# Rotary embedding from cached tables: the sums of one row block move from TensorE to POOL, the first store follows them, and the spread table halves are copied whole

## The chip, the cores and the metric

The kernel runs on one core of a Trainium2 chip. A core has TensorE (PE in the profile, with its weight loads as PEld), VectorE (DVE), ScalarE (ACT), GpSimd (POOL) and SyncE (SP), which here only issues transfers, and 16 DMA engines that all transfers share. The metric is device time in microseconds (us), the median of several executions. A profile is a record of one more execution; its span runs from the first to the last recorded instruction, and the execution's own time is a little longer.

## The reference

`x` has shape (8, 8, 1024, 64) in float32: 8 x 8 heads, 1024 positions, 64 channels. `cos_cached` and `sin_cached` have one row of 32 values for each position.

```
x_first, x_second = x[..., :32], x[..., 32:]
out_first  = x_first * cos - x_second * sin
out_second = x_first * sin + x_second * cos
out = concatenate([out_first, out_second], axis=-1)
```

So each half of each row is multiplied by both tables, and the four products are combined in two sums. Input and output have 16.8 MB each, the tables 0.13 MB each.

## The kernel before, in words

**Tiles.** `x` is cut into 8 tiles x0 to x7 of 128 partitions by 4096 elements (2 MB). A partition holds 64 rows of 64 channels, so 16 partitions in a row cover the 1024 positions of one head, and the tables needed repeat every 16 partitions. All eight tiles stay in SBUF, and results are written in place. `s` is a second tile of the same size (three buffers in turn) for the sine products.

**Loads.** SP issues the sine table and then all of x, in order: x0 in two halves, x1 to x7 whole (lines 55 to 63). ScalarE's queue takes the cosine table (line 56). The transfers report on a small set of semaphores that are used in turn, so that a later transfer can have to wait until the earlier one with the same semaphore has landed.

**Tables.** `sn` and `cs` must hold, in every partition, the 64 table rows which its 64 rows of x need. They are loaded into `raw` as 32 blocks of 32 rows, one block (1024 elements) to a partition. A partition of x needs two neighbouring blocks: an even one for its rows 0 to 32, an odd one for its rows 32 to 64. The odd blocks come from a shuffle on DVE and six copies of 32 partitions on POOL and ScalarE (lines 136 to 141). The even table blocks are spread to 128 partitions by matmuls with the 0/1 matrix `sel` into PSUM (line 134): four matmuls of 512 columns, sine and cosine for rows 0 to 16 (half 0 of the block), then for rows 16 to 32 (half 1). Each result is a PSUM tile of its own: n0, c0, n1, c1.

**The first tile, x0.** Its rows 0 to 32 are multiplied by DVE with the tables straight from those PSUM tiles (lines 142 to 146): four products, s and x for rows 0 to 16, then for rows 16 to 32. ScalarE meanwhile copies rows 32 to 64 of x0 to PSUM (`stage`, tiles pre0 and pre1) and then the four PSUM tables to `sn` and `cs` (lines 150 to 152). DVE multiplies the staged rows with `products`. The sums of rows 16 to 32, 32 to 48 and 48 to 64 are made by POOL (`pool_sums`), in that order; those of rows 0 to 16 are left to TensorE.

**The rest.** x2 is computed by POOL alone (`on_pool`, twice 32 rows). Tiles 1, 3, 4, 5, 6 and 7 are cut into chunks of 24, 24 and 16 rows: 18 chunks, 0 to 17. For each, ScalarE copies x to PSUM (`stage`, two staging tiles `st` in turn), and DVE makes both products (`products`). The sums are made in one of three ways:

- by DVE itself, for the chunks in `alone`;
- by POOL (`pool_sums`), for those in `behind`;
- by TensorE (`pe_sums`), in groups of 16 rows, ten of them in `on_pe`: four matmuls with plus or minus the unit matrix add the products in the one PSUM tile `acc`, and ScalarE copies the result back to x (`pe_back`).

**Order.** The order on each engine is written out by hand. In the loop over the chunks (lines 205 to 214), chunk c's products are written first, then the staging copy of chunk c + 2, then, if c is in `back_after`, the copy back of the TensorE group that is running and the matmuls of the next, and last what stands for c in `behind`: stores and POOL sums. A group's matmuls need `acc`, so they wait for the copy back of the group before. ScalarE thus alternates between staging copies, which wait for DVE to be done with a staging tile, and copies back, which wait for TensorE.

**Stores.** x0, x1 and the last quarter of x7 go out on ScalarE's queue, x2 to x6 and the rest of x7 on SP's. A store waits on its queue for all parts of its tile, and what is behind it on that queue waits with it. "Store 0" below is that of x0, and so on.

Of the kernel before, what the change touches and what calls it, by code (L numbers as in the profile page):

```python
# [8 lines left out]
def kernel(  # L9
# [7 lines left out]
    nc = tc.nc  # L17
    fp32 = mybir.dt.float32
    TT = mybir.AluOpType
    P = nc.NUM_PARTITIONS  # L20
# [7 lines left out]
    BK = 512  # L28
    G = BK // half
    Q = 32  # L30
    H = R // 2
    C = H * half
# [13 lines left out]
    cs = const.tile([P, T], fp32, name="cs")  # L46
    sn = const.tile([P, T], fp32, name="sn")
    sel = const.tile([Q, P], fp32, name="sel")
# [27 lines left out]
    def rows(t, n0, n1):  # L76
        return t[:, n0 * hd:n1 * hd].rearrange("p (n k j) -> p n k j", k=2, j=half)

    def tab(t, n0, n1):
        v = t[:, n0 * half:n1 * half].rearrange("p (n o j) -> p n o j", o=1, j=half)  # L80
        return v.to_broadcast([P, n1 - n0, 2, half])

    def mul(eng, o, a, t):
        eng.tensor_tensor(out=o, in0=a, in1=t, op=TT.mult)  # L84

    def sums(eng, o, c, s):
        eng.tensor_tensor(out=o[:, :, 0], in0=c[:, :, 0], in1=s[:, :, 1], op=TT.subtract)  # L87
        eng.tensor_tensor(out=o[:, :, 1], in0=c[:, :, 1], in1=s[:, :, 0], op=TT.add)  # L88
# [3 lines left out]
    def s_of(u):  # L92
        if u not in sv:
            sv[u] = tv.tile([P, F], fp32, name="s", tag="s")
        return sv[u]

    def stage(pt, u, n0, n1):
        nc.scalar.copy(out=pt[:, :(n1 - n0) * hd], in_=xt[u][:, n0 * hd:n1 * hd])  # L98

    def products(pt, u, n0, n1, alone=False):  # L100

        xr, sr, pr = rows(xt[u], n0, n1), rows(s_of(u), n0, n1), rows(pt, 0, n1 - n0)
        mul(nc.vector, sr, pr, tab(sn, n0, n1))
        mul(nc.vector, pr if alone else xr, pr, tab(cs, n0, n1))
        if alone:
            sums(nc.vector, xr, pr, sr)
# [8 lines left out]
    def pool_sums(u, n0, n1):  # L115
        xr = rows(xt[u], n0, n1)
        sums(nc.gpsimd, xr, xr, rows(s_of(u), n0, n1))

    def store(q, u, n0=0, n1=R):
        q.dma_start(out=of[u][:, n0 * hd:n1 * hd], in_=xt[u][:, n0 * hd:n1 * hd])  # L120
# [5 lines left out]
    with ExitStack() as first:  # L126
        p0, p1, p2 = [first.enter_context(tc.tile_pool(name=n, bufs=1, space=PS))
                      for n in ("p0", "p1", "p2")]
        even = [[p0.tile([P, BK], fp32, name="n0"), p0.tile([P, BK], fp32, name="n1")],
                [p0.tile([P, BK], fp32, name="c0"), p1.tile([P, BK], fp32, name="c1")]]  # L130
        pre = [p1.tile([P, 2 * BK], fp32, name="pre0"), p2.tile([P, 2 * BK], fp32, name="pre1")]
        for i in range(2):
            for part, r in zip(even, (rs, rc)):
                nc.tensor.matmul(part[i], sel, r[:, i * BK:(i + 1) * BK],  # L134
                                 start=True, stop=True)
        odd = [2 * (i % (Q // 2)) + 1 for i in range(Q)]
        for t, r in ((sn, rs), (cs, rc)):
            nc.vector.stream_shuffle(t[0:Q, C:], r, odd)  # L138
        for t, k, eng in ((sn, 1, 0), (sn, 2, 1), (sn, 3, 0), (cs, 1, 1), (cs, 2, 0), (cs, 3, 1)):
            f = nc.gpsimd.tensor_copy if eng else nc.scalar.copy  # L140
            f(out=t[k * Q:(k + 1) * Q, C:], in_=t[0:Q, C:])  # L141
        for i in range(2):
            n0, n1 = i * G, (i + 1) * G
            xr = rows(xt[0], n0, n1)
            mul(nc.vector, rows(s_of(0), n0, n1), xr, tab(even[0][i], 0, G))
            mul(nc.vector, xr, xr, tab(even[1][i], 0, G))
        pool_sums(0, G, H)
        for i in range(2):
            stage(pre[i], 0, H + i * G, H + (i + 1) * G)
        for i in range(2):  # L150
            for t, part in ((sn, even[0]), (cs, even[1])):
                nc.scalar.copy(out=t[:, i * BK:(i + 1) * BK], in_=part[i])
        for i in range(2):
            n0, n1 = H + i * G, H + (i + 1) * G
            products(pre[i], 0, n0, n1)
            pool_sums(0, n0, n1)
# [7 lines left out]
    def pe_sums(u, n0):  # L164
        xr, sr = rows(xt[u], n0, n0 + G), rows(s_of(u), n0, n0 + G)
        for k in range(2):
            nc.tensor.matmul(a[:, k], plus, xr[:, :, k], start=True, stop=False)  # L167
            nc.tensor.matmul(a[:, k], plus if k else minus, sr[:, :, 1 - k],  # L168
                             start=False, stop=True)

    def pe_back(u, n0):
# [7 lines left out]
    cuts = ((0, 24), (24, 48), (48, 64))  # L179
    chunks = [(u, n0, n1) for u in (1, 3, 4, 5, 6, 7) for n0, n1 in cuts]  # L180
    alone = {(1, 48), (5, 48), (7, 24), (7, 48)}
    on_pe = [(0, 0), (1, 0), (1, 16), (1, 32), (3, 0), (3, 16), (4, 0), (4, 16), (5, 0), (6, 0)]
    back_after = (0, 1, 3, 5, 6, 8, 10, 11, 13, 15)
    behind = {
        0: [(store, nc.scalar, 0)],
        5: [(store, nc.scalar, 1), (pool_sums, 3, 32, 64)],
        8: [(store, nc.sync, 3), (pool_sums, 4, 32, 64)],
        10: [(pool_sums, 5, 16, 48)],
# [8 lines left out]
    def put(c):  # L197
        if c < len(chunks):
            u, n0, n1 = chunks[c]
            stage(st[c % 2], u, n0, n1)  # L200

    put(0)
    put(1)
    pe_sums(*on_pe[0])
    for c, (u, n0, n1) in enumerate(chunks):
        products(st[c % 2], u, n0, n1, (u, n0) in alone)
        put(c + 2)
        if c in back_after:
            i = back_after.index(c)
# [34 lines left out]
```

## Time and profile before

| What | Value |
|---|---|
| Time, median of 6 executions | 86.93 us (86.51 to 87.24) |
| The profiled execution's own time | 87.03 us |
| Its span | 84.2 us |
| DVE busy | 71.2 us (85%) |
| POOL busy | 63.5 us (75%) |
| PE busy | 47.7 us (57%) |
| ACT busy | 41.7 us (49%) |
| Bytes moved by DMA | 33.83 MB, mean 402 GB/s |
| DVE's last instruction | starts at 75.60 us, 0.68 us long |
| Issue of stores 0 and 1 | 23.85 and 38.57 us |
| Issue of stores 2 to 6 | 47.76, 52.38, 60.68, 65.48 and 70.28 us |
| Issue of the two stores of x7 | 72.75 and 76.31 us |

Busy time is time with an instruction in execution on an engine. In lists of instructions in order of time a line gives the start, the duration, the engine, the line of the kernel, the operation, what is written and read, the number of merged records, and in brackets the idle time before it with what ended it. The row by slices has 40 slices of the span; a digit is the busy share in tenths, 9 standing for 90% or more.

### The profile page before, as it was taken

To read this page: it belongs to the slowest core of one execution; us is meant where nothing else is said; L and a number is where in the kernel's file an instruction comes from. 1 tells how busy PE (TensorE), PEld (TensorE's weight loads), DVE (VectorE), ACT (ScalarE), POOL (GpSimd) and SP (SyncE) were. 2 spreads that over 40 slices of the span, in tenths; PEclk is the share of its full clock that TensorE was granted. 3 is DMA by queue.
4 is the path that set the end of the run, shared out by engine and by line. 5 is a ranking of instruction groups with operands and counts; after the bars stand their busy time and mean duration, and the time that the engine had idled before them with its cause. 6 is when DMAs were issued, how large, how long until landed. Compare 5 with 4: busy or idle time off the path is not lost.

```text
span 84.2 us, 434 instructions
## 1 busy us (share of the span) xinstructions
PE 47.7 (57%) x88; PEld 18.2 (22%) x88; DVE 71.2 (85%) x56; ACT 41.7 (49%) x39; POOL 63.5 (75%) x37
## 2 busy tenths in 40 slices
PE   0199920089769494966949496299495980000000
PEld 0143200034133241413324141134140420000000
DVE  0198879999999999999999999999999999992000
ACT  4359795903372964685288544660675763000000
POOL 5049009999999999999999999999979999400000
PEclk9999999999999999999999999955999999655555
DMA  2999999999989999999999999999999999999980
GB/s 31 304 416 463 405 436 436 420 451 389 475 381 381 358 444 420 436 436 420 444 412 459 412 459 389 459 412 444 428 428 436 420 447 405 451 420 422 438 364 18
DMA packets 2691, 33.83 MB, mean 402 GB/s; under 512 B 321, under 2 KB 321, under 8 KB 513
## 3 DMA queue, kind: packets, MB, share of 16 engines
q1 hardware_dynamic: 2208, 28.97, 82.5%
q10 hardware_dynamic: 480, 4.85, 13.6%
q14 instruction: 3, 0.02, 0.0%
HBM read 17.04 MB, written 16.78 MB: 401 GB/s over the span
## 4 chain that ended last, share of the span: by engine, by line
DVE 47%; issue 2%; ACT 1%; DVEq 1%
DVE s L84 21%; DVE x L84 18%; DVE st L84 5%; DVE x L87 2%; DVE x L88 2%; ACT st L98 1%; DVEq L239 1%
## 5 line engine op out<-in xcount | busy, mean ns | idle before, releaser
L167 PE MATMUL acc<-x,plus 128*128 128x512 f32 x40 | 23.4, 670 | 17.5 <-ACT x L172 11.4
L98 ACT COPY st<-x 128x1536 f32<-128x1536 f32 (+1 forms) x18 | 23.4, 1302 | 13.3 <-DVE x L84 10.2
L84 DVE TENSOR_TENSOR s<-st,sn 128x1536 f32<-128x1536 f32 (+1 forms) x18 | 28.3, 1570 | 0.0
L84 DVE TENSOR_TENSOR x<-st,cs 128x1536 f32<-128x1536 f32 (+1 forms) x14 | 22.9, 1634 | 0.0
L87 POOL TENSOR_TENSOR x<-x,s 128x512 f32<-128x512 f32 (+2 forms) x9 | 16.3, 1814 | 4.4 <-issue 4.0
L88 POOL TENSOR_TENSOR x<-x,s 128x512 f32<-128x512 f32 (+2 forms) x9 | 16.3, 1809 | 0.0
L172 ACT COPY x<-acc 128x1024 f32<-128x1024 f32 x10 | 10.1, 1011 | 10.9 <-PE acc L168 10.9
L167 PEld LDWEIGHTS acc<-x,plus 128*128 128x128 f32 x40 | 7.6, 210 | 32.4 <-ACT x L172 18.9
L168 PE MATMUL acc<-s,minus 128*128 128x512 f32 x20 | 12.0, 685 | 0.0
L168 PE MATMUL acc<-s,plus 128*128 128x512 f32 x20 | 10.2, 593 | 0.0
L84 POOL TENSOR_TENSOR x<-x,cs 128x2048 f32<-128x2048 f32 x2 | 9.1, 4543 | 0.2
L84 POOL TENSOR_TENSOR g<-x,sn 128x2048 f32<-128x2048 f32 x2 | 9.1, 4544 | 0.1
L134 PE MATMUL n<-raw,sel 32*128 32x512 f32 x4 | 3.9, 1089 | 3.9 <-DMA raw<-in_sin_cached_dram 3.9
L84 DVE TENSOR_TENSOR st<-st,cs 128x1024 f32<-128x1024 f32 (+1 forms) x4 | 5.4, 1356 | 0.0
L168 PEld LDWEIGHTS acc<-s,minus 128*128 128x128 f32 x20 | 4.2, 211 | 5.3 <-issue 5.3
L168 PEld LDWEIGHTS acc<-s,plus 128*128 128x128 f32 x20 | 4.0, 198 | 5.3 <-issue 5.3
L87 POOL TENSOR_TENSOR x<-x,g 128x1024 f32<-128x1024 f32 x2 | 4.7, 2354 | 0.2
L88 POOL TENSOR_TENSOR x<-x,g 128x1024 f32<-128x1024 f32 x2 | 4.7, 2354 | 0.0
L134 PE MATMUL c<-raw,sel 32*128 32x512 f32 x4 | 3.8, 1056 | 0.0
L141 POOL COPY sn<-sn 32x1024 f32<-32x1024 f32 x1 | 1.0, 1029 | 3.4 <-DVE sn L138 3.4
L141 ACT COPY sn<-sn 32x1024 f32<-32x1024 f32 x2 | 2.1, 1043 | 2.4 <-DVE sn L138 2.4
L138 DVE LOAD_MASK_SELECT sn<-raw x1 | 0.0, 14 | 3.8 <-DMA raw<-in_sin_cached_dram 3.8
(26 smaller groups left out, 31.3 us busy)
## 6 DMA issues: line engine op xcount, KB each, us to landing
x<-in_x_dram SPq DMA_DIRECT2D x7, 2048.0 KB, 26.6
out_dram<-x SPq DMA_DIRECT2D x5, 2048.0 KB, 8.0
out_dram<-x ACTq DMA_DIRECT2D x2, 2048.0 KB, 13.8
x<-in_x_dram SPq DMA_DIRECT2D x2, 1024.0 KB, 6.3
out_dram<-x SPq DMA_DIRECT2D x1, 1536.0 KB, 9.7
out_dram<-x ACTq DMA_DIRECT2D x1, 512.0 KB, 6.9
raw<-in_cos_cached_dram ACTq DMA_DIRECT2D x1, 128.0 KB, 3.4
raw<-in_sin_cached_dram SPq DMA_DIRECT2D x1, 128.0 KB, 3.1
```

The costliest lines, as they stand in the source:

```text
L84: eng.tensor_tensor(out=o, in0=a, in1=t, op=TT.mult)
L87: eng.tensor_tensor(out=o[:, :, 0], in0=c[:, :, 0], in1=s[:, :, 1], op=TT.subtract)
L88: eng.tensor_tensor(out=o[:, :, 1], in0=c[:, :, 1], in1=s[:, :, 0], op=TT.add)
L98: nc.scalar.copy(out=pt[:, :(n1 - n0) * hd], in_=xt[u][:, n0 * hd:n1 * hd])
L134: nc.tensor.matmul(part[i], sel, r[:, i * BK:(i + 1) * BK], start=True, stop=True)
L141: f(out=t[k * Q:(k + 1) * Q, C:], in_=t[0:Q, C:])
L167: nc.tensor.matmul(a[:, k], plus, xr[:, :, k], start=True, stop=False)
L168: nc.tensor.matmul(a[:, k], plus if k else minus, sr[:, :, 1 - k], start=False, stop=True)
L172: nc.scalar.copy(out=rows(xt[u], n0, n0 + G), in_=a.rearrange("p k n j -> p n k j"))
L239: with _tile.TileContext(nc) as tc:
```

## The change

Four things change:

- The spread sine and cosine blocks are one PSUM tile each (`n` and `c`, 1024 columns) instead of four tiles. The matmuls of half 0 are written ahead of DVE's products as before, those of half 1 behind DVE's products and POOL's sums for rows 0 to 16 (`spread`).
- POOL also makes the sums of rows 0 to 16 of x0, ahead of its others. The TensorE group (0, 0) is gone from `on_pe`, with its copy back; the matmuls of (1, 0) are started behind chunk 0.
- ScalarE copies each spread table in one instruction of 1024 columns instead of two of 512.
- Store 0 is written ahead of the loop over chunks, behind the first two staging copies on ScalarE. It then waits for POOL's sums alone, not for a copy back.

In the built program the matmuls of half 1 wait for DVE: the sine one for the first of DVE's products, the cosine one for the second. The load of x7, which waited for the second half of x0's load, now waits for x1's load, and the load of x4 waits for the cosine table's.

```diff
-        even = [[p0.tile([P, BK], fp32, name="n0"), p0.tile([P, BK], fp32, name="n1")],
-                [p0.tile([P, BK], fp32, name="c0"), p1.tile([P, BK], fp32, name="c1")]]
-        pre = [p1.tile([P, 2 * BK], fp32, name="pre0"), p2.tile([P, 2 * BK], fp32, name="pre1")]
-        for i in range(2):
+        even = [p0.tile([P, C], fp32, name=n) for n in "nc"]
+        pre = [p.tile([P, 2 * BK], fp32, name="pre") for p in (p1, p2)]
+
+        def spread(i):
             for part, r in zip(even, (rs, rc)):
-                nc.tensor.matmul(part[i], sel, r[:, i * BK:(i + 1) * BK],
+                nc.tensor.matmul(part[:, i * BK:(i + 1) * BK], sel, r[:, i * BK:(i + 1) * BK],
                                  start=True, stop=True)
...
+        spread(0)
         for i in range(2):
             n0, n1 = i * G, (i + 1) * G
             xr = rows(xt[0], n0, n1)
-            mul(nc.vector, rows(s_of(0), n0, n1), xr, tab(even[0][i], 0, G))
-            mul(nc.vector, xr, xr, tab(even[1][i], 0, G))
-        pool_sums(0, G, H)
+            mul(nc.vector, rows(s_of(0), n0, n1), xr, tab(even[0], n0, n1))
+            mul(nc.vector, xr, xr, tab(even[1], n0, n1))
+            pool_sums(0, n0, n1)
+            if i == 0:
+                spread(1)
         for i in range(2):
             stage(pre[i], 0, H + i * G, H + (i + 1) * G)
-        for i in range(2):
-            for t, part in ((sn, even[0]), (cs, even[1])):
-                nc.scalar.copy(out=t[:, i * BK:(i + 1) * BK], in_=part[i])
+        for t, part in ((sn, even[0]), (cs, even[1])):
+            nc.scalar.copy(out=t[:, :C], in_=part)
...
-    on_pe = [(0, 0), (1, 0), (1, 16), (1, 32), (3, 0), (3, 16), (4, 0), (4, 16), (5, 0), (6, 0)]
-    back_after = (0, 1, 3, 5, 6, 8, 10, 11, 13, 15)
+    on_pe = [(1, 0), (1, 16), (1, 32), (3, 0), (3, 16), (4, 0), (4, 16), (5, 0), (6, 0)]
+    back_after = (1, 3, 5, 6, 8, 10, 11, 13, 15)
     behind = {
-        0: [(store, nc.scalar, 0)],
+        0: [(pe_sums, 1, 0)],
...
     put(0)
     put(1)
-    pe_sums(*on_pe[0])
+    store(nc.scalar, 0)
     for c, (u, n0, n1) in enumerate(chunks):
```

## The prediction

> **What bounds the kernel now.** I read the chain of waits first. It ends on DVE and gives it 47% of the span, which would make VectorE the bound. The row by slices of the page does not agree:
>
> ```profile
> span 84.2 us, 434 instructions
> ...
> DVE  0198879999999999999999999999999999992000
> ...
> DMA  2999999999989999999999999999999999999980
> GB/s 31 304 416 463 405 436 436 420 451 389 475 381 381 358 444 420 436 436 420 444 412 459 412 459 389 459 412 444 428 428 436 420 447 405 451 420 422 438 364 18
> ```
>
> DVE stops about six slices before the end; the DMA engines are at 9 from the second slice to the last but one. Nothing idles on that side until the bytes are through: 33.83 MB at some 430 GB/s is 78.7 us, and with 1.7 us before the first packet and about 2 us from the last packet to the span's end that is nearly all of 84.2. The edges, in the table by stretches (us, then busy time of PE, PEld, DVE, ACT, POOL, then TensorE clock, DMA share, GB/s):
>
> ```profile
> 26.00:28.00 2.00, 1.53 (x4) 0.38 (x2) 2.00 (x3) 0.43 (x1) 2.00 (x1) 1.00 1.03 295
> 60.00:62.00 2.00, 1.34 (x3) 0.68 (x4) 2.00 (x3) 1.55 (x3) 1.55 (x1) 1.00 1.01 434
> 76.00:82.00 6.00, 0.00 (x0) 0.00 (x0) 0.28 (x1) 0.00 (x0) 0.00 (x0) 0.50 0.97 408
> 82.00:83.00 1.00, 0.00 (x0) 0.00 (x0) 0.00 (x0) 0.00 (x0) 0.00 (x0) 0.50 0.17 66
> ```
>
> From 76.3 us on no engine computes, and the DMA engines still work off a backlog until just past 82.
>
> So a change moves the end only if it makes the DMA engines idle, starts them at another time, or changes what a byte costs. Where are they near to idling? Stores 4, 5 and 6 (tiles x4, x5, x6) are issued at 60.68, 65.48 and 70.28 by SP, and the stores ahead of them land at 63.4, 68.2 and 73.5. Store 3's sixteen closing packets (under 512 B) pass between 62.25 and 63.0, so its data ends there, 62.6 in the mean. An issue needs 1.0 us to its first packet: the first one starts at 0.74, and in the DMA view of 1 to 3 us (0.05 us a digit) the first busy digit stands at 1.75:
>
> ```profile
> DMA  0000000000000009997970014924959896999239
> ```
>
> Store 4 can thus move from 61.7 on, 0.6 us before the first engine needs it, 0.9 before the mean one. By the same sum (landing less 0.8, issue plus 1.0) stores 5 and 6 have 0.9 and 1.4. That is the kernel's slack: less than a microsecond of delay at store 4. Earlier stores have more (store 2 is issued at 47.76, while the last load lands at 53.7).
>
> **What the Trainium skill says.** "DMA: Bandwidth & Descriptors", section "Issuing engines are not separate DMA queues": stores from SP and ACT run on the same 16 engines and interleave. The trace agrees: with ACT's queue active the rate stays at 418 (30 to 32 us). So an earlier store on ACT is no new bandwidth. Its section "Queues, rings and completion order" has each engine take turns between queues that have work; a store beside the loads therefore takes half the rate from them. "TensorE: Matmul & The Clock Gate", section "What's actually happening": the clock halves after an idle window of about 3.4 us, and the window runs freely. Here an idle time of only 2.26 us was enough once:
>
> ```profile
> 38.59 1.13 PE L167 MATMUL acc<-x,plus 128*128 128x512 f32 x2 [1.46 <-ACT x L172]
> ...
> 54.16 1.16 PE L167 MATMUL acc<-x,plus 128*128 128x512 f32 x2 [2.26 <-ACT x L172]
> 55.12 1.90 PE L168 MATMUL acc<-s,minus 128*128 128x512 f32 x2
> ```
>
> After 1.46 us the group ran at full speed, after 2.26 us it took 1.90 us instead of 1.02 a pair, with the clock at 0.5 from 55 to 58.5. A warm group takes 3.70 us (23.83 to 27.53), the cold one 5.39 (54.16 to 59.55).
>
> **The change, part by part.**
>
> *Head.* The sine spreads of both halves now share a tile, the cosine ones too, and the second pair of matmuls is written behind DVE's first products. In the built program it waits for DVE: the sine one for the first product, the cosine one for the second. Now:
>
> ```profile
> 6.57 1.22 DVE L84 TENSOR_TENSOR s<-x,n 128x1024 f32<-128x1024 f32 x1 [0.20 <-DMA x<-in_x_dram]
> 7.49 1.91 PE L134 MATMUL n<-raw,sel 32*128 32x512 f32 x2
> 9.44 1.22 DVE L84 TENSOR_TENSOR s<-x,n 128x1024 f32<-128x1024 f32 x1 [0.33 <-PE n L134]
> 11.14 1.22 DVE L84 TENSOR_TENSOR x<-x,c 128x1024 f32<-128x1024 f32 x1 [0.49 <-PE c L134]
> ```
>
> The first product ends at 7.79; PE followed DVE elsewhere by 0.22 us (16.90 to 17.12), so the sine matmul starts at 8.0 instead of 7.49 (7.8 if the signal cost nothing). The cosine matmul is ready at 9.33 but queues behind it until 9.7. DVE waits for each, so its third and fourth products start at 9.95 and 11.65: **DVE is 0.5 us late** (0.3 to 0.6) and, busy without a gap afterwards, carries that to the end: 76.3 becomes 76.8. What hides it is the DMA backlog and the slack of 0.6 to 0.9 above; without them it would cost its 0.5.
>
> *POOL.* Its new group of sums (two instructions of 1.26 us) fits in its idle 3.97 us before 12.51: rows 0 to 16 are ready at 9.11, so it runs from 9.3 to 11.8. The next group waits for DVE's fourth product, now ending at 12.87: it starts at 13.0 instead of 12.51. POOL is then full, so its 0.5 us passes to x2 and x3: store 2 at 48.3, store 3 at 52.9. Both join a queue that has loads until 53.7 and store 2 until 58.5: nothing.
>
> *Table copies.* Four of about 0.6 us (2.38) become two; a copy of 128x1024 from PSUM takes 1.01 (L172), so 2.02. The second waits for DVE's fourth product (12.87) and ends near 13.95. The copy behind it on ScalarE waited for x1's load until 13.93: it shifts by less than 0.1, and DVE needs its result at 17.3. Zero.
>
> *Store 0 and the removed group.* PE loses 4 matmuls (17.15 to 22.72), ScalarE the copy back of 1.01 us. Store 0 waits on ScalarE for POOL's last sums of x0, 19.87 plus 0.5: issue at 20.4 instead of 23.85. Behind it queues the copy of chunk 2, which waits for DVE until 20.8 anyway (20.31 now), and DVE wants it at 24: nothing. DMA-wise, 2 MB move up by 3.4 us and the loads behind move back. ACT's queue got its first packets some 4 us after its issue (3 of them by 28.0), so it takes half from 24.3 to about 33.7; x3 (landing 23.6) is clear, x4 slips from 30.5 to about 33, and ScalarE wants it at 34.4. x5 and later land as before, the sum of bytes being the same. Also, x7's load now waits on SP for x1's landing (13.8) instead of leaving at 8.96; behind it are only stores from 48 us on, ahead of it four to five loads of 4.9 us. Nothing.
>
> *PE and ScalarE from 20 to 40 us.* Group (1, rows 0) runs from 21.0, cold after ten idle us, to 26.4, not 27.5, and its copy back follows chunk 3's. From then on ScalarE is set by DVE: the copy back of (1, 16) stands behind chunk 5's copy (31.6 plus 0.5), so (1, 32) runs 33.1 to 36.8; its copy back stands behind chunk 7's (until 38.1), so (3, 0) starts at 39.1. Everything later is the old time plus 0.5: store 1 39.1, store 4 61.2, 5 66.0, 6 70.8. Store 4's first packet is then due at 62.2, just ahead of 62.25.
>
> Sum against the profiled execution: 0 at the start, 0 at store 4 (0 to 0.2 if its latency is longer than 1.0), 0 at the end, as the last store (76.8) joins a backlog to 82. Span 84.2 to 84.4; around the span it has 2.8 us (87.03 less 84.2). That execution is 0.1 above the median of 86.93, so I take **87.0 us**; with small terms both ways 86.6 to 87.3.
>
> **Rivals.**
>
> *Slower: two cold groups.* (3, 0) has PE idle from 36.8 to 39.1, 2.3 us, as much as the gap of 2.26 that halved the clock. Cold costs it 1.7: its copy back comes at 44.5, not 42.8, chunk 9's copy behind it at 45.5 and ready at 46.9, where DVE wants it at 45.4: DVE loses 1.5. If (4, 16) is also cold, as it is in the trace before, store 4 is issued at 60.68 + 0.5 + 1.5 = 62.7 and moves at 63.7; the DMA engines idle 1.1 us: **88.0**. It decides from a delay of about 1.3 us at store 4. With one of the two warm, store 4 comes between 61.0 and 61.2 and nothing shows. For: the size of the gap. Against: it takes both, and a gap that falls across two clock windows leaves each with two thirds busy, as the 1.1 us gaps do unharmed.
>
> *Faster: the slow stretch goes.* From 26 to 28 us only 295 GB/s moved, a loss of 2 x (1 - 295/430) = 0.63 us, just before store 0's first packets; store 1 has none. If an earlier store avoids it: **86.3**. Against: it will still be the first write.
>
> *DVE is the bound after all* (the chain of waits): the 0.5 shows in full, **87.4**. Against: six idle slices. *The earlier store is a gain at the end*, 3.4 us: **83.5**. Against: no idle DMA time to fill.
>
> **How the numbers follow.** 0.5% (0.43 us) is about what a measurement can tell from no change. Forecast 0.56; two cold groups 0.25; slow stretch gone 0.10; DVE bound 0.04; earlier end 0.02; unnamed gain 0.03. Faster 0.15, same 0.56, slower 0.29. The range reaches from near the second rival to just above the first, 86.4 to 88.1.
>
> **What would show it.** DVE's third product near 9.95; DVE's end near 76.8; store 0 issued near 20.4; DMA slices at 9 throughout; store 4 near 61.2. Wrong if the DMA row dips near 62, or the stretch of 295 GB/s is gone.

## The result, and the profile after

| Kernel | Executions | Median, us | Lowest to highest, us |
|---|---|---|---|
| before | 69 | 86.88 | 86.05 to 87.69 |
| after | 34 | 87.47 | 85.96 to 88.11 |

The 34 executions of the changed kernel fall into two groups with nothing between them: 15 from 85.96 to 86.51 and 19 from 87.43 to 88.11. The stated ratio of the two kernels, **0.9928 (0.9908 to 0.9948)**, leaves out executions more than 1.5% above a kernel's fastest, and so the whole upper group. By it the change makes the kernel 0.7% faster; the median over all executions is 0.7% above that of before. Both are true of this kernel: it is a bit faster in four executions of nine, and slower in five. The span of each execution, that is, the time from the first to the last recorded instruction, is on record too: 83.8 to 84.4 us in the lower group, 85.3 to 86.0 us in the upper one. What lies outside the span, the time less the span, is the same in both, 2.06 to 2.19 us. Two things have to be explained, then: why the lower group is faster than before, and where the upper group's longer span comes from.

The changed kernel's profiled execution is one of the lower group, at 86.14 us. From its page, the span, the row of DVE, the TensorE clock and the two DMA rows by slices:

```profile
span 84.0 us, 417 instructions
...
DVE  0298679999999999999999999999999999994000
...
PEclk9999999999999999999999999965999999755555
DMA  2999999999989999989899999999999999999980
GB/s 37 330 437 437 421 452 398 468 390 476 390 328 421 413 460 398 476 382 491 382 484 390 437 429 413 460 406 460 398 476 390 468 394 437 437 413 419 439 357 10
```

The picture is the old one: DVE stops well before the end, the DMA engines run through. The span is 84.0 us, 84.2 before. But the time is 86.14 against 87.03: **what lies outside the span is 2.14 us in this execution, 2.8 in the profiled one of before.** Inside, the instructions in order of time show the change doing what was worked out:

```profile
7.69 2.07 PE L134 MATMUL n<-raw,sel 32*128 32x512 f32 x2 [0.25 <-DVE s L84]
9.80 1.22 DVE L84 TENSOR_TENSOR s<-x,n 128x1024 f32<-128x1024 f32 x1 [0.84 <-PE n L134]
11.51 1.22 DVE L84 TENSOR_TENSOR x<-x,c 128x1024 f32<-128x1024 f32 x1 [0.49 <-PE c L134]
20.19 0.37 ACTq L120 DMA_DIRECT2D out_dram<-x  x1
38.95 1.12 PE L170 MATMUL acc<-x,plus 128*128 128x512 f32 x2 [2.32 <-ACT x L175]
54.52 1.40 PE L170 MATMUL acc<-x,plus 128*128 128x512 f32 x2 [2.26 <-ACT x L175]
55.72 1.92 PE L171 MATMUL acc<-s,minus 128*128 128x512 f32 x2
76.67 0.34 ACTq L120 DMA_DIRECT2D out_dram<-x  x1
```

The second sine matmul waits for DVE, DVE waits for it, and the last store leaves 0.36 us later than before (76.31). Store 0 leaves at 20.19. Before group (3, 0), at 38.95, PE now idles 2.32 us instead of 1.46. In this execution that group still runs warm (at the full clock, about 1.0 us a pair of matmuls), and only (4, 16) is cold (at the halved clock, 1.92 us a pair), as in the profile of before.

### The profile page after: what moved, and what is told of

The parts are those of the page before. It is cut to its first block, busy times and chain, and to the rows that moved or that the text cites. A ratio compares the mean times of both kernels' runs of the same rounds, so it can differ in the third digit from the quotient of the medians.

```text
span 84.0 us, 417 instructions
## 1 busy us (share of the span) xinstructions
PE 44.3 (53%) x80; PEld 16.5 (20%) x80; DVE 71.2 (85%) x56; ACT 40.7 (48%) x36; POOL 66.0 (79%) x39
## 4 chain that ended last, share of the span: by engine, by line
DVE 72%; DMA 6%; issue 5%; PE 5%; ACT 1%; DVEq 1%; SPq 0%
DVE s L84 33%; DVE x L84 28%; DMA x<-in_x_dram 6%; DVE st L84 6%; DVE x L87 3%; DVE x L88 3%; PE n L134 2%; PE c L134 2%; ACT st L98 1%; DVEq L242 1%; SPq L55 0%; DVEq L84 0%
## 5 line engine op out<-in xcount | busy, mean ns | idle before, releaser
L170 PE MATMUL acc<-x,plus 128*128 128x512 f32 x36 | 21.2, 673 | 21.3 <-ACT x L175 11.9
L87 POOL TENSOR_TENSOR x<-x,s 128x512 f32<-128x512 f32 (+2 forms) x10 | 17.5, 1751 | 2.6 <-DVE x L84 1.2
L88 POOL TENSOR_TENSOR x<-x,s 128x512 f32<-128x512 f32 (+2 forms) x10 | 17.5, 1747 | 0.0
L170 PEld LDWEIGHTS acc<-x,plus 128*128 128x128 f32 x36 | 6.8, 210 | 34.8 <-ACT x L175 18.5
L175 ACT COPY x<-acc 128x1024 f32<-128x1024 f32 x9 | 9.1, 1010 | 7.8 <-PE acc L171 7.8
L171 PE MATMUL acc<-s,minus 128*128 128x512 f32 x18 | 11.0, 696 | 0.0
L171 PE MATMUL acc<-s,plus 128*128 128x512 f32 x18 | 9.2, 592 | 0.0
L84 DVE TENSOR_TENSOR s<-x,n 128x1024 f32<-128x1024 f32 x2 | 2.4, 1220 | 1.2 <-PE n L134 0.8
L87 DVE TENSOR_TENSOR x<-st,s 128x512 f32<-128x512 f32 (+1 forms) x4 | 3.0, 758 | 0.1
```

Of the source, the lines that this page charges most:

```text
L175: nc.scalar.copy(out=rows(xt[u], n0, n0 + G), in_=a.rearrange("p k n j -> p n k j"))
```

## The experiments

All of them in one table; the kernels with the same letter ran on one chip together and share their executions of the kernel before. The changed kernel itself was not run again in any of these sets. "Outside" is time less span, of each execution. The ratio is made as the one above, with its 95% interval; where a kernel has an upper group, the median and the range tell more.

| Kernel | Executions | Median, us | Range, us | Outside, us: median (range) | Ratio to before |
|---|---|---|---|---|---|
| b_again (a) | 19 | 86.73 | 86.31 to 87.75 | 2.73 (2.31 to 3.12) | 1.0038 (1.0007 to 1.0068) |
| b_pool (a) | 22 | 86.24 | 86.01 to 87.51 | 2.13 (2.06 to 2.17) | 0.9994 (0.9957 to 1.0030) |
| b_spread (a) | 13 | 86.84 | 86.44 to 88.06 | 2.72 (2.10 to 3.10) | 1.0057 (1.0018 to 1.0096) |
| a_backfirst (a) | 14 | 86.06 | 85.94 to 86.38 | 2.13 (2.07 to 2.18) | 0.9971 (0.9948 to 0.9993) |
| a_first5 (b) | 16 | 86.17 | 85.94 to 86.45 | 2.12 (2.07 to 2.19) | 0.9943 (0.9923 to 0.9963) |
| a_first10 (b) | 22 | 87.14 | 86.01 to 87.59 | 2.12 (2.06 to 2.19) | 1.0001 (0.9966 to 1.0037) |
| bf_4more (b) | 22 | 86.31 | 85.96 to 89.37 | 2.25 (2.07 to 3.13) | 0.9941 (0.9915 to 0.9968) |
| b_4less (b) | 22 | 86.14 | 85.77 to 86.58 | 2.02 (1.87 to 2.14) | 0.9937 (0.9918 to 0.9957) |
| a_first10_13 (c) | 22 | 86.20 | 85.92 to 86.81 | 2.11 (2.07 to 2.19) | 0.9951 (0.9931 to 0.9971) |
| bf_8more (c) | 22 | 86.66 | 86.07 to 88.98 | 2.15 (2.07 to 3.06) | 0.9983 (0.9956 to 1.0011) |
| bf_act4 (c) | 22 | 86.49 | 85.95 to 88.94 | 2.13 (2.08 to 2.20) | 0.9959 (0.9935 to 0.9983) |
| a_cold34 (c) | 4 | 88.89 | 87.60 to 89.19 | 2.09 (2.08 to 2.10) | 1.0216 (1.0136 to 1.0297) |
| b_pe4less (d) | 13 | 86.17 | 85.91 to 86.66 | 2.00 (1.89 to 2.14) | 0.9941 (0.9922 to 0.9961) |
| b_pe2less (d) | 9 | 86.27 | 85.88 to 86.65 | 1.98 (1.92 to 2.08) | 0.9947 (0.9921 to 0.9974) |
| b_4more (d) | 21 | 86.89 | 86.04 to 87.45 | 2.05 (1.91 to 3.07) | 0.9997 (0.9971 to 1.0024) |
| a_first5_10_13 (d) | 6 | 86.08 | 86.02 to 86.46 | 2.16 (2.08 to 2.18) | 0.9940 (0.9917 to 0.9963) |

The executions of before that belong to them have medians of 86.87 (a), 86.73 (b), 86.69 (c) and 86.72 (d). Set a's has one at 85.65, so that its executions above 86.93 are left out of the ratio, and before looks better in these four ratios than its median does: b_again, the same kernel, comes out at 1.0038.

### Which part of the change does it, and is it outside the span?

**b_again** is the kernel before, unchanged.

> The kernel before, unchanged, run again to see the span beside the time of each execution. If the 0.6 us that the changed kernel is faster by in its better executions lies outside the span (2.14 us there, 2.83 in the one execution of before that is known), every execution of this one has time less span near 2.8 us, whatever its span. If it lies inside, time less span is 2.1 to 2.2 in most executions and the spans themselves reach from 83.9 to 85.5.

Neither side is quite right: time less span isn't fixed but spreads from 2.31 to 3.12 here, and from 1.85 to 3.14 in the executions of before of set a. But the difference is there: the median outside is 2.73, against 2.13 in the changed kernel, while the median span is 84.0, against 84.1 in the changed kernel's lower group.

**b_pool** is before with the moved sums alone:

```diff
-        pool_sums(0, G, H)
+            pool_sums(0, n0, n1)        # in the loop over the two halves
...
-    on_pe = [(0, 0), (1, 0), (1, 16), ...
+    on_pe = [(1, 0), (1, 16), ...
-        0: [(store, nc.scalar, 0)],
+        0: [(pe_sums, 1, 0)],
...
-    pe_sums(*on_pe[0])
+    store(nc.scalar, 0)
```

> The kernel before with only the moved sums: POOL makes rows 0 to 16 of x0, group (0, 0) is gone from TensorE and store 0 follows POOL; the spread tables stay in four tiles and four copies. If the moved sums make both the gain and the two groups, this one has two groups at 86.2 and 87.6 as the whole change has. If the gain comes from the shared spread tile and the copies, it lies near 86.9. DVE is not late here, so by the slack argument a doubly cold execution costs 0.4 less than in the whole change: 87.2.

**b_spread** is the other half of the diff alone: the shared spread tiles, `spread` and the two whole table copies, with group (0, 0) left on TensorE.

> The kernel before with only the shared spread tile and the two whole table copies; group (0, 0) stays on TensorE. DVE is 0.4 us late from its third product on. If the moved sums make the gain, this one is at 86.9 to 87.2, never a gain; if the spread and the copies make it, it is near 86.2.

The moved sums make both effects: in b_pool, outside is 2.06 to 2.17 in every execution, and 13 of 22 lie at 86.01 to 86.32, 9 at 86.80 to 87.51. The spread and the copies gain nothing: b_spread's median is 86.84 against 86.87, with outside as before, and its ratio of 1.0057 can't be told from b_again's 1.0038. A cost of theirs may show in the upper group: without DVE's delay it lies around 87.1 in b_pool instead of the 87.6 of the whole change, close to the 0.4 less that was expected.

### What is outside the span?

The DMA view of 84.5 to 87 us, behind the span's end, of the kernel before:

```profile
DMA packets 2, 0.02 MB, mean 10 GB/s; under 512 B 0, under 2 KB 0, under 8 KB 0
...
q8 instruction: 1, 0.02, 3.2%
q14 instruction: 1, 0.01, 1.0%
```

The same view of the kernel after:

```profile
DMA packets 2, 0.02 MB, mean 7 GB/s; under 512 B 0, under 2 KB 0, under 8 KB 0
...
q14 instruction: 2, 0.02, 1.6%
```

An instruction fetch on a queue of its own, q8, a single packet of 16 KB (3.2% of 16 engines for 2.5 us: 1.3 us), stands behind the end of the work before, and in b_again and b_spread; it is absent after. (The smaller fetches on q14 are in both.) The Trainium skill, "Runtime: NRT & Kernel Launch", section "Instruction fetch mechanics", says that programs are refilled in blocks of 16 KiB and that the cost of crossing a boundary is mostly hidden. The change takes four matmuls and a copy back out of two programs, so I tried whose length matters.

**b_4less** leaves out the last TensorE group instead of the first, at the other end of the kernel:

```diff
-    on_pe = [(0, 0), (1, 0), ... (5, 0), (6, 0)]
-    back_after = (0, 1, 3, 5, 6, 8, 10, 11, 13, 15)
+    on_pe = [(0, 0), (1, 0), ... (5, 0)]
+    back_after = (0, 1, 3, 5, 6, 8, 10, 11, 13)
```

> The kernel before without its last TensorE group: the four matmuls of (6, 0) and their copy back are left out, so rows 0 to 16 of x6 are not summed. Nothing at the head changes, and store 0 stays where it was. If the length of TensorE's program makes the gain, time less span is 2.14 and the median 86.1 to 86.3. If the gain needs the earlier store or the sums on POOL, time less span stays near 2.7 and the time near 86.7.

Outside falls to 2.02 and the time to 86.14, with nothing moved at the head. So the gain needs neither the earlier store nor POOL's sums. **b_pe4less** and **b_pe2less** keep the copy back and leave out four or two of the matmuls of that group only:

```diff
     def pe_sums(u, n0):
+        if u == 6:                                   # b_pe4less
+            return
...
-        for k in range(2):
+        for k in range(1 if u == 6 else 2):          # b_pe2less
```

> The kernel before with the four matmuls of its last TensorE group (6, 0) left out and nothing else: the copy back stays and copies what the group before left (rows 0 to 16 of x6 come out wrong). If TensorE's program alone decides what lies outside the span, time less span is 1.9 to 2.2 and the time 86.0 to 86.3. If it took the copy back, POOL or the stores too, it stays near 2.7.

> The same with only two of the four matmuls left out (the second half of each row in rows 0 to 16 of x6 comes out wrong). A boundary within these last instructions gives either 2.1 or 2.7 in nearly all executions; a cost that grows with the length gives about 2.4.

Both are at 2.0: in the kernel before, TensorE's program alone does it, and two matmuls are enough. It is a step, not a slope. **b_4more** makes the program of before longer:

```diff
             if i + 1 < len(on_pe):
                 pe_sums(*on_pe[i + 1])
+            else:
+                pe_sums(*on_pe[i])
```

> The kernel before with four matmuls more behind its last TensorE group, their result dropped. If a longer TensorE program is worse, time less span is 2.7 or above. If the end of the program falls on a boundary of the instruction fetch in the kernel before, four matmuls more move the boundary into the kernel, where nothing waits for it, and time less span falls to about 2.1.

Outside falls again, to 2.05 in the median, 20 of 21 executions at or below 2.22. And its trace has the fetch within the work, between 67 and 69 us, among the stores:

```profile
q1 hardware_dynamic: 68, 0.85, 102.2%
q8 instruction: 1, 0.02, 2.9%
```

What fits these runs is that, before, the end of TensorE's program falls just past a block's boundary, and the last block is fetched when everything else is over. No view shows the boundary itself. The late fetch costs about 0.6 us, so here the crossing is not hidden. Dropping a group moves the end back across the boundary.

A longer program is not as good as a shorter one, though: b_4more gains no time, as its span is 84.7 in the median against 84.1 in its set's executions of before. Its trace suggests why. The fetch keeps one of the 16 DMA engines from the stores for 0.93 us (2.9% of 16 engines for 2 us). At the end of the transfers the stretch from 82.75 to 83.75 us is empty before:

```profile
82.75:83.75 1.00, 0.00 (x0) 0.00 (x0) 0.00 (x0) 0.00 (x0) 0.00 (x0) 0.50 0.00 0
```

The same stretch of b_4more:

```profile
82.75:83.75 1.00, 0.00 (x0) 0.00 (x0) 0.00 (x0) 0.00 (x0) 0.00 (x0) 0.50 0.07 29
```

A share of 0.07 of 16 engines is about one engine at work for that microsecond, and the span is 85.2. One engine seems to run behind with its part of the stores by about the time of the fetch. The slow stretch from 26 to 28 us is deeper there too, 188 GB/s instead of 295. All this was read from one trace and not tested by a run.

**bf_4more** puts four matmuls back, result dropped, into a variant of the changed kernel (a_backfirst, which the next section describes), **bf_8more** eight, and **bf_act4** lengthens ScalarE's program instead:

```diff
+    pe_sums(0, 0)                       # bf_4more and bf_8more, ahead of store 0
     store(nc.scalar, 0)
...
+            else:
+                pe_sums(*on_pe[i])      # bf_8more, behind the last group
...
-    nc.scalar.mul(minus, plus, -1.0)
+    for _ in range(5):                  # bf_act4
+        nc.scalar.mul(minus, plus, -1.0)
```

> The variant with the early copies back (median 86.06, time less span 2.14), with TensorE's four matmuls for rows 0 to 16 of x0 put back where they were, their result dropped. TensorE's program is as long as before the change; ScalarE's, POOL's and the stores' stay as they are. If what lies outside the span depends on the length of TensorE's program, time less span goes back to 1.9 to 3.1, mean 2.7, the span stays at 83.9 to 84.2, the time is near 86.6, and a 16 KB packet stands behind the span's end. If it came with the moved sums in another way (the order of the stores, the semaphores), time less span stays at 2.14 and the time at 86.1.

> The variant with the early copies back, with eight TensorE matmuls more whose result is dropped: four where group (0, 0) was and four behind the last group, where PE is done. If a longer TensorE program brings the instruction fetch behind the end of the work, time less span is above 2.4 in most executions (eight of 22 with four more matmuls), near 2.7, and the 16 KB instruction packet shows behind the span. If the length of TensorE's program has nothing to do with it, time less span is 2.14 in most.

> The variant with the early copies back, with ScalarE's first small instruction (minus the unit matrix) made five times instead of once, in its idle time before 4.9 us. ScalarE's program is then one instruction longer than in the kernel before. If the length of ScalarE's program brings the late fetch, time less span rises to 2.4 to 3.1; if only TensorE's does, it stays at 2.14 and the time at 86.1.

ScalarE's length doesn't matter: outside stays at 2.08 to 2.20. With four matmuls back, the value above 2.4 returns in 8 of 22 executions only, with eight in 3 of 22. Neither fits a boundary that the number of matmuls sets by itself: bf_4more has as many of them as the kernel before, bf_8more as many as b_4more, and yet the profiled executions of both have no packet on q8 at all, within the work or behind it. So putting the matmuls back into the changed kernel did not bring the late fetch back in most executions. What else decides, and why a single execution has the late fetch or not, stays open.

### Where the upper group comes from

**a_backfirst** is the changed kernel with two copies back ahead of the staging copies behind chunks 5 and 10, so that PE's 2.3 us of idle time before groups (3, 0) and (4, 16) go down to 1.1. **a_first5** has this behind chunk 5 only, **a_first10** behind chunk 10 only, and two more have other lists:

```diff
-        put(c + 2)
+        if c not in (5, 10):       # (5,), (10,), (10, 13), (5, 10, 13)
+            put(c + 2)
         if c in back_after:
             i = back_after.index(c)
             pe_back(*on_pe[i])
+            if c in (5, 10):
+                put(c + 2)
```

> The changed kernel, but behind chunks 5 and 10 ScalarE copies the TensorE sums back before it stages the next chunk, so that PE's idle time before groups (3, 0) and (4, 16) falls from 2.3 to 1.1 us. If the upper group of executions (87.6 us) comes from those two groups running cold, it is gone: all executions near 86.2, median 86.1 to 86.4, and the clock stays at 1.0 until PE is done. If the upper group has another cause (the order of the loads, a transfer state), about half of the executions stay at 87.6.

> The changed kernel with the early copy back behind chunk 5 only: PE's idle time before group (3, 0) falls from 2.3 to 1.1 us, that before (4, 16) stays at 2.26. If the upper group of executions takes both groups cold, or (3, 0) cold, it is gone here: all near 86.1 to 86.4. If (4, 16) cold is enough by itself, about half of the executions stay above 87.

> The changed kernel with the early copy back behind chunk 10 only: (3, 0) keeps its idle time of 2.3 us and can run cold, (4, 16) has 1.1 us and is warm. By the prediction's rival both must be cold to cost anything, so all executions are near 86.1 to 86.4. If (3, 0) cold is enough by itself, executions above 87 remain.

With (3, 0)'s idle time at 1.1 us the upper group is gone: none of 14 in a_backfirst, none of 16 in a_first5, although the latter leaves PE 2.95 us idle before (4, 16). With only (4, 16) helped, a_first10, it is there: 13 of 22 at 87.05 or above. Its profiled execution, at 87.39, is one of them, so it shows what happens in this variant. In order of time, from group (3, 0) on:

```profile
39.11 1.12 PE L170 MATMUL acc<-x,plus 128*128 128x512 f32 x2 [2.06 <-ACT x L175]
...
40.07 1.72 PE L171 MATMUL acc<-s,minus 128*128 128x512 f32 x2
41.59 1.92 PE L170 MATMUL acc<-x,plus 128*128 128x512 f32 x2
44.54 1.01 ACT L175 COPY x<-acc 128x1024 f32<-128x1024 f32 x1 [3.58 <-PE acc L171]
45.45 2.82 ACT L98 COPY st<-x 128x1536 f32<-128x1536 f32 x2
46.94 1.76 DVE L84 TENSOR_TENSOR s<-st,sn 128x1536 f32<-128x1536 f32 x1 [1.43 <-ACT st L98]
...
66.45 1.13 PE L170 MATMUL acc<-x,plus 128*128 128x512 f32 x2 [2.74 <-ACT x L175]
68.97 1.92 PE L170 MATMUL acc<-x,plus 128*128 128x512 f32 x2
71.89 1.01 ACT L175 COPY x<-acc 128x1024 f32<-128x1024 f32 x1 [1.25 <-PE acc L171]
72.97 0.33 SPq L120 DMA_DIRECT2D out_dram<-x  x1
```

The same copy back and the same product in the profile of after:

```profile
42.69 1.01 ACT L175 COPY x<-acc 128x1024 f32<-128x1024 f32 x1 [1.89 <-PE acc L171]
...
45.27 1.75 DVE L84 TENSOR_TENSOR s<-st,sn 128x1536 f32<-128x1536 f32 x1
```

In a_first10, PE idles 2.06 us, the clock halves, a pair takes 1.92 us, the copy back comes at 44.54 (42.69 after), the staging copy of chunk 9 behind it at 45.45, and DVE waits 1.43 us, where it did not wait at all in the profile of after. A second cold group, (6, 0), makes store 6 wait until 72.97 (70.6 after). By stretches of 1 us, with the DMA share and GB/s last:

```profile
71.00:72.00 1.00, 0.85 (x2) 0.01 (x1) 1.00 (x2) 0.11 (x1) 1.00 (x2) 1.00 1.19 508
72.00:73.00 1.00, 0.00 (x0) 0.00 (x0) 0.96 (x2) 0.90 (x1) 1.00 (x2) 1.00 0.05 16
73.00:74.00 1.00, 0.00 (x0) 0.00 (x0) 1.00 (x2) 0.00 (x0) 1.00 (x1) 1.00 0.62 262
```

The DMA engines stand still for more than a microsecond, and the span is 85.3. Is one cold group enough? **a_first10_13** takes away the idle time before (6, 0) too.

> The changed kernel with the early copy back behind chunks 10 and 13: (3, 0) keeps its idle time of 2.1 to 2.3 us and runs cold in some executions, but no later group has more than 1.8 us of idle time before it. If one cold group only uses up the slack of the stores and a second one is needed to make the DMA engines idle, all executions are near 86.0 to 86.5, some with a lower clock. If (3, 0) cold is enough by itself, about half of them stay at 87.1 to 87.6.

The upper group is gone: all 22 at or below 86.81 (on another chip than a_first10, however). The profiled execution is that highest one, and (3, 0) is cold in it. DVE's stall, in order of time:

```profile
47.60 1.76 DVE L84 TENSOR_TENSOR s<-st,sn 128x1536 f32<-128x1536 f32 x1 [1.43 <-ACT st L98]
```

And one stretch of 1 us, later:

```profile
72.00:73.00 1.00, 0.00 (x0) 0.00 (x0) 1.00 (x1) 0.33 (x1) 1.00 (x1) 0.50 0.01 0
```

Store 6 came at 72.41 and the DMA engines ran empty for a while: 84.7 of span, 0.6 above this kernel's median of 84.1. The stall has only a part in that. In this execution everything was late by some 0.8 us before it (store 1 issued at 39.75, at 38.93 after), since the sine table came a microsecond later (DVE's first shuffle at 4.62, at 3.59 after). So one cold group together with a late start cost 0.6; what it costs by itself is not shown. **a_cold34** forces two, by leaving PE 7.98 us idle before (3, 0) and 6.89 us before (4, 16):

```diff
     def pe_sums(u, n0):
+        if (u, n0) in ((1, 32), (4, 0)):
+            return
```

> The changed kernel with the matmuls of groups (1, 32) and (4, 0) left out and their copies back kept (rows 32 to 48 of x1 and 0 to 16 of x4 come out wrong), so that PE idles over 7 us before (3, 0) and (4, 16) and both run cold in every execution. If two cold groups make the upper group of executions of the changed kernel, all executions are at 87.4 or above, DVE waits 1.4 us or more ahead of chunk 9, store 4 is issued at 62.6 or later, and the DMA row dips near 63 us. If cold groups don't cost time, it stays near 86.2.

All four executions are at 87.60 or above. DVE's wait, in order of time:

```profile
47.89 1.76 DVE L84 TENSOR_TENSOR s<-st,sn 128x1536 f32<-128x1536 f32 x1 [2.56 <-ACT st L98]
```

Store 4 is issued at 64.23 instead of 61.04; the stretches around it:

```profile
62.00:63.00 1.00, 1.00 (x3) 0.19 (x1) 1.00 (x1) 0.00 (x0) 0.00 (x0) 1.00 0.01 0
63.00:64.00 1.00, 0.11 (x1) 0.00 (x0) 1.00 (x2) 0.85 (x1) 0.00 (x0) 1.00 0.00 0
64.00:65.00 1.00, 0.79 (x2) 0.49 (x3) 0.90 (x1) 1.00 (x2) 0.00 (x0) 1.00 0.00 0
```

Three microseconds without a byte moved. This is the rival of the prediction, made certain: two cold groups, a late store 4, idle DMA engines. It is stronger than it can be in the changed kernel, since PE starts both groups cold instead of losing its clock within them (2.56 us of stall, 1.43 in a_first10). So the run shows the chain of causes, and not that it makes the 1.4 us of the changed kernel's upper group.

For the changed kernel itself no trace of an upper execution exists. That its cold groups are (3, 0) and then (4, 16) is inferred: from the idle times of 2.32 and 2.26 us, from the mean clock over the span (0.889 to 0.896 in the upper group, 0.905 to 0.925 in 13 of the 15 lower ones), and from a_first5, where the upper group is gone with the long idle time before (3, 0) alone taken away. The other two lower executions, at 86.38 and 86.51, have a mean clock of 0.887: it counts where the clock is lost, not only how long. The trace of b_pool shows that too: group (1, 32) is cold there, behind 2.11 us of idle time, and the execution, at 86.03, is one of its fastest.

**a_first5_10_13** leaves PE no idle time above 1.75 us between groups.

> The changed kernel with the early copy back behind chunks 5, 10 and 13. No idle time of PE before a group is above 1.8 us. If two cold groups need longer gaps than that, all executions are at 85.9 to 86.5, median 86.1, 0.8 to 0.9% below the kernel before. If gaps of 1.6 to 1.8 us can also halve the clock twice, some executions stay above 87.

Six executions, all in the lower group: 86.02 to 86.46, median 86.08 against 86.72, ratio 0.9940 (0.9917 to 0.9963). PE's clock and the DMA engines by slices:

```profile
PEclk9999999999999999999999999999999998555555
DMA  3999999999999999999999999999999999999980
```

The first group, at 21.23, still takes 2.05 us for its first pair, where the row has a 9; from its end on the clock holds until PE is done. Together with a_first5 (16 executions, none above 86.45) this version beats the kernel before and has no upper group. Six executions are few, though, and a warning stands beside them: bf_4more and bf_act4, which have the order of a_backfirst with its 2.95 us of idle time before (6, 0), had 7 and 6 executions of 22 with spans above 85, where a_backfirst had none of 14. They ran on other chips than a_backfirst. Whether the chip has a part in how often a group runs cold was not tested.

## Why the prediction was right or wrong

**The step that failed is the one that turned the span into a time:** "Span 84.2 to 84.4; around the span it has 2.8 us". The span was right (84.0 in the profiled execution, 83.8 to 84.4 in the lower group). The 2.8 us were taken over from one execution as if a change could not touch them. They measured 2.14 in the profiled execution after, 2.13 in the median of all 34, against 2.73 in b_again. In the kernel before, two TensorE matmuls less are enough for that (1.98), so TensorE's shorter program is the likely cause after the change too. That is about the whole gain of the lower group (86.2 in the median, 86.88 before). With 2.14 the same span would have given 86.3 to 86.5. The trace held a hint: it shows instruction fetches as a kind of DMA packet of its own, and I read only as far as the span reaches.

**The slower rival fits 19 of 34 executions, and was given 0.25.** Its chain is the one that the variants show: (3, 0) loses its clock, its copy back holds up the staging copy of chunk 9, DVE stalls by 1.43 us in a_first10 (1.5 forecast), a second cold group makes a store late, and the DMA engines run dry. That store is number 6 in a_first10, where the second cold group is (6, 0), and number 4, as forecast, in a_cold34; which it is in the changed kernel no trace shows. Its size was 1.1 us; the two groups' medians lie 1.4 apart. Two of its terms were off. That "nothing shows" with one of the two warm is too strong: DVE's stall also delays store 6, whose slack of 1.4 the prediction had and did not use again, and in a_first10_13 one cold group and a start late by 0.8 cost 0.6. And the chance of 0.25 was low: in the traces of all these kernels, 13 of 19 idle times between 2.05 and 2.95 us ended in a cold group. A forecast of one number could not have held here in any case: the kernel has two times.

**Right, by their numbers:**

| Step | Forecast | Measured after |
|---|---|---|
| DVE's third and fourth product | 9.95 and 11.65 | 9.80 and 11.51 |
| DVE's end | 76.8 | 76.64 |
| store 0 issued | 20.4 | 20.19 |
| PE idle before (3, 0) | 2.3 | 2.32 |
| stores 4, 5, 6 issued | 61.2, 66.0, 70.8 | 61.0, 65.8, 70.6 |

All times are a little early since the first transfers came 0.25 us earlier in this execution (DVE's first shuffle at 3.59 instead of 3.84). DMA stays at 9 in nearly every slice, so the earlier store, the two whole copies and POOL's extra sums are worth nothing inside the span, as the sum had it. The first sum of the prediction was loose, though: 78.7, 1.7 and 2 us make 82.4, not 84.2, and the slow stretch explains 0.6 of the rest. The forecast doesn't rest on it.

**The other rivals.** The slow stretch did not go away: it moved along with store 0, now the slice of 328 GB/s at about 24 us, as the prediction's own objection had it. DVE as the bound is refuted: it ends 0.36 later and the span is not longer. The earlier store brought nothing at the end.

## What to carry to other kernels

When transfers fill a span, count what is near to emptying them and what lies outside the span; compute time is then only slack. When the time changes and the span doesn't, look in the trace behind the last instruction. Whether a program's length is the cause is cheap to test by adding or dropping a few instructions elsewhere. Where an engine has a clock that drops after idle time, an order that lengthens its waits can give a kernel two times: put the copies that it waits for ahead of work that can wait, as a_first5_10_13 does.

## What was unexpected of the hardware

- A block of instructions fetched behind the end of the work took 1.2 to 1.3 us for 16 KB and made the time about 0.6 us longer. Two matmuls less took it away. With four more it came within the work, took 0.93 us, and the time was no shorter.
- PE's clock halved after an idle time of 2.05 us in one trace, while 2.32 and 2.95 us left it alone in others. Of the idle times between groups, none up to 1.91 us ended in a cold group; of those from 2.05 to 2.95 us, 13 of 19 did. The Trainium skill, "TensorE: Matmul & The Clock Gate", section "What's actually happening", speaks of an idle window of about 3.4 us that runs freely; here less idle time than that was often enough.
- A store that joined a full DMA backlog on the other queue moved its first packets some 4 us after its issue (issue 23.85, three packets by 28.0 us), not in turn at once.
